# Key normalisation by pairs of heads, gate constants in their own memory, and two later places for small TensorE work in a one-core encoder layer

## The chip, the core and the metric

The kernel runs on one core of one Trainium2 chip. The metric is the device time of one execution in microseconds (us). The core's engines work side by side, each through a queue of its own in order: TensorE (PE) multiplies matrices and transposes; VectorE (DVE), ScalarE (ACT) and GpSimd (POOL) work on elements; SyncE (SP) issues most DMA transfers. An engine waits for another by semaphores.

## The reference

One layer of a hybrid encoder is computed for 1024 new frames and for 64 further frames of a stream with 512 cached ones; everything is float32.

```python
h = rms_norm(x, g_norm1) * (1 + scale1) + shift1
c_q, c_kv, k_rope_raw, gq, gk, gv, g_lr, g_r = split(h @ w_in)
# latent attention: 4 heads, key of 128 + 64 rotary, value of 128
latent = concat(past_latent, rms_norm(c_kv, g_kv_lora))
kv = (latent @ w_ukv).reshape(B, S, 4, 128 + 128)      # k_nope, v
k = concat(k_nope, krope);  k = rms_norm(k, g_k_head);  k = concat(k[:128], rope(k[128:]))
a_out = chunk_causal_attention(q, k, v)
# gated linear attention
log_a = log_sigmoid(g_lr @ w_gate_up + b_gate_up) / 16
b_out, s_new = gla(gq, gk, gv, log_a, s0), gated by silu(g_r)
x = x + gate1 * (concat(a_out, b_out) @ w_out)
h2 = rms_norm(x, g_norm2) * (1 + scale2) + shift2
x = x + gate2 * (square(relu(h2 @ w_up)) @ w_down)
```

## The kernel before, in words

Tokens lie along the free axis where a projection is multiplied, 1088 of them in chunks of 384, 384 and 320, later in halves of 544 and quarters of 272. Precise products are made by `mm3` (L94 to L96): each operand is split into a high and a low part, and three fast matmuls (high x high, low x high, high x low) are added in PSUM. The splitting is done by ACT (high part, a cast, L102) and DVE (low part, a subtraction, L103 and L106). PSUM is handed out in three groups of banks, named in the profile by the tile that a matmul writes: `mm` (four), `tp` (two) and `g` (two).

The stages follow one another with much overlap: the modulation vectors (`mod_vec`, L177), the first norm and the input projection; the gated linear attention (from about 90 us); the keys of the past and the queries (265 to 360 us); attention with the keys of the new tokens made along the way (to some 560 us); the output projection and the second norm (to 700 us); the MLP.

What a stage emits is decided by `interleave`. Streams are generators that yield three things: an estimate of PE time, a delay before they may go on, and a condition. `interleave` lets the first ready stream go on and moves a model clock. So the delays (`yield 0, 4500, None`, in model nanoseconds) say how much other work goes between two steps of a stream. The tile framework then sets the order within each engine's queue by an estimate of its own, so an edit in one place can move instructions in others.

Keys and values (`keys_values`, L960): for a tile of 128 tokens two products of the latent with the matrix `UK`, each for two heads, go into two `g` banks. From each, DVE copies the keys to `kn` (L982) and the values to `v` (L985), and ACT squares the keys and adds them up (L984, two per product). After both, POOL adds epsilon and the rotary part's square (L988) and raises to the power -1/2 (L989) for all four heads at once; DVE multiplies the keys (`kn`, L991) and the rotated part (`krt`, L992) by it, 128x512 each. Later, after the delay in L995, PE transposes `kn` (L998, four heads) and then `krt` (L1005). The function is used for four past tiles (t = 0 to 3), for the 64 new tokens of the running stream (`new_keys(8)`), both in `past_keys`, and for the eight tiles of new keys.

The gate of the linear attention: `wg` holds `w_gate_up` with its bias in row 96, and `glrT` the transposed low-rank input with a row of ones. Both are zeroed by POOL, and `wg`, its bias and the small indicator matrix `indi` are loaded, when the pool `big` is opened, whose memory is that of earlier tiles (L613 to L625). L653 transposes the input (from DVE's copy L650), L654 copies it into `glrT`, and L657 multiplies.

The second norm (`norm2`, L1471 to L1506) works on the four column blocks of 272 tokens in turn. `main` evicts each of the eight rows of the output projection with the residual added (L1456), ACT squares it (L1460, L1463) and DVE adds the squares to `acc` (L1464). After a delay (L1473) PE sums `acc` over partitions (L1478), DVE and POOL make the reciprocal root (L1481, L1482), DVE puts it on diagonals (L1485), and after a second delay PE broadcasts it (L1489).

## Time and profile before

| what | value |
|---|---|
| median of 3 runs | 1357.65 us (1357.14 to 1358.04) |
| profiled execution | 1358.17 us |
| its span, first to last instruction | 1356.4 us |
| mean granted TensorE clock | 0.996 |
| busy: PE, DVE, ACT, POOL | 1325.8, 894.9, 655.3, 64.5 us |
| DMA | 183.64 MB, mean 135 GB/s |

A row of the groups view has line, engine, operation, output <- input, shapes and count, then busy time and mean nanoseconds of one, then the idle time of the engine just before with what ended it. A row of the timeline has the start, the duration and in brackets the idle time before with its releaser. A row of the waits has the waiting engine and tile, the releaser, and us in total, times and the longest. A row of the windows has the stretch, its length, the busy time of PE, weight loads, DVE, ACT and POOL with counts, the granted clock, the DMA share and GB/s. Durations of pipelined matmuls overlap, so starts tell more than lengths.

### The profile page before, as it was taken

To read this page: it belongs to the slowest core of one execution; us is meant where nothing else is said; L and a number is where in the kernel's file an instruction comes from. 1 tells how busy PE (TensorE), PEld (TensorE's weight loads), DVE (VectorE), ACT (ScalarE), POOL (GpSimd) and SP (SyncE) were. 2 spreads that over 40 slices of the span, in tenths; PEclk is the share of its full clock that TensorE was granted. 3 is DMA by queue.
4 is the path that set the end of the run, shared out by engine and by line. 5 is a ranking of instruction groups with operands and counts; after the bars stand their busy time and mean duration, and the time that the engine had idled before them with its cause. 6 is when DMAs were issued, how large, how long until landed. Compare 5 with 4: busy or idle time off the path is not lost.

```text
span 1356.4 us, 25887 instructions
## 1 busy us (share of the span) xinstructions
PE 1325.8 (98%) x10052; PEld 1257.9 (93%) x10052; DVE 894.9 (66%) x1926; ACT 655.3 (48%) x1634; POOL 64.5 (5%) x110
## 2 busy tenths in 40 slices
PE   9999999989999999999989999999999999999998
PEld 8899999878867788999989999999999999999998
DVE  4898787465576656677799565665636865874554
ACT  5465545443255656753575445444443333433432
POOL 0110010121111100000000000000000000000000
PEclk9999999999999999999999999999999999999999
DMA  9420123324445320573417443444349845543441
GB/s 343 137 74 1 48 76 90 107 83 126 153 129 171 96 89 16 163 209 111 137 40 232 141 156 128 160 139 138 115 168 341 282 152 192 162 125 92 132 124 34
DMA packets 155110, 183.64 MB, mean 135 GB/s; under 512 B 16063, under 2 KB 106475, under 8 KB 154987
## 3 DMA queue, kind: packets, MB, share of 16 engines
q1 hardware_dynamic: 147530, 176.44, 41.0%
q10 hardware_dynamic: 7456, 5.54, 1.3%
q8 instruction: 79, 1.29, 0.4%
q14 instruction: 45, 0.36, 0.1%
HBM read 130.71 MB, written 51.23 MB: 134 GB/s over the span
## 4 chain that ended last, share of the span: by engine, by line
PE 82%; DVE 7%; DMA 4%; ACT 4%; POOL 2%; issue 1%; SPq 0%; ACTq 0%; DVEq 0%; POOLq 0%
PE mm L94 14%; PE mm L96 13%; PE mm L95 13%; PE g L94 6%; PE g L96 6%; PE g L95 6%; PE tp L94 3%; PE tp L95 3%; PE tp L96 3%; PE mm L1076 3%; PE g L1103 2%; PE mm L177 1%; PE g L881 1%; PE tp L1113 1%; POOL ssk L989 1%
## 5 line engine op out<-in xcount | busy, mean ns | idle before, releaser
L102 ACT CAST opers<-quad 128x512 fp32r<-128x512 f32 x112 | 69.4, 620 | 184.6 <-PE mm L96 145.1
L103 DVE TENSOR_TENSOR opers<-quad,opers 128x512 fp32r<-128x512 f32 x112 | 77.2, 690 | 112.3 <-ACT opers L102 112.3
L96 PE MATMUL mm<-opers 128*128 128x272 f32 x448 | 128.9, 288 | 0.0
L94 PE MATMUL mm<-opers 128*128 128x272 f32 x448 | 128.6, 287 | 0.3 <-DVE e L1910 0.3
L95 PE MATMUL mm<-opers 128*128 128x272 f32 x448 | 128.3, 286 | 0.0
L94 PE MATMUL mm<-ah,wh 128*128 128x272 f32 x424 | 122.5, 290 | 2.0 <-ACT wh L102 1.7
L95 PE MATMUL mm<-al,wh 128*128 128x272 f32 x424 | 121.8, 288 | 0.3 <-DVE al L103 0.3
L96 PE MATMUL mm<-ah,wl 128*128 128x272 f32 x424 | 121.6, 288 | 0.0
L94 PE MATMUL mm<-hh,wh 128*128 128x384 f32 (+2 forms) x264 | 90.6, 344 | 0.7 <-ACT wh L321 0.7
L95 PE MATMUL mm<-hl,wh 128*128 128x384 f32 (+2 forms) x264 | 87.2, 330 | 0.0
L96 PE MATMUL mm<-hh,wl 128*128 128x384 f32 (+2 forms) x264 | 86.9, 330 | 0.0
L94 PEld LDWEIGHTS mm<-opers 128*128 128x128 f32 x448 | 84.6, 189 | 0.5 <-issue 0.5
L96 PEld LDWEIGHTS mm<-opers 128*128 128x128 f32 x448 | 84.3, 188 | 0.0
L95 PEld LDWEIGHTS mm<-opers 128*128 128x128 f32 x448 | 84.1, 188 | 0.0
L94 PEld LDWEIGHTS mm<-ah,wh 128*128 128x128 f32 x424 | 80.0, 189 | 3.1 <-ACT wh L102 2.2
L95 PEld LDWEIGHTS mm<-al,wh 128*128 128x128 f32 x424 | 79.8, 188 | 0.5 <-DVE al L103 0.5
L96 PEld LDWEIGHTS mm<-ah,wl 128*128 128x128 f32 x424 | 79.8, 189 | 0.0
L103 DVE TENSOR_TENSOR opers<-ru,opers 128x544 fp32r<-128x544 f32 x108 | 77.6, 719 | 2.2 <-ACT opers L102 2.0
L102 ACT CAST opers<-ru 128x544 fp32r<-128x544 f32 x108 | 69.4, 643 | 13.1 <-PE mm L96 11.7
L102 ACT CAST wh<-ru 128x512 fp32r<-128x512 f32 x67 | 41.1, 618 | 65.7 <-PE g L95 24.6
L103 DVE TENSOR_TENSOR wl<-ru,wh 128x512 fp32r<-128x512 f32 x67 | 45.9, 689 | 35.5 <-ACT wh L102 35.3
L94 PE MATMUL mm<-wh,hh 128*128 128x264 f32 (+3 forms) x216 | 65.9, 305 | 0.0
(410 smaller groups left out, 4241.5 us busy)
## 6 DMA issues: line engine op xcount, KB each, us to landing
ru<-u_d SPq DMA_DIRECT2D x108, 272.0 KB, 2.9
raw<-in_w_ada SPq DMA_DIRECT2D x40, 512.0 KB, 4.2
ru<-in_w_up SPq DMA_DIRECT2D x32, 512.0 KB, 4.1
quad<-in_w_down SPq DMA_DIRECT2D x16, 1024.0 KB, 7.2
u_d<-st SPq DMA_DIRECT2D x60, 272.0 KB, 2.1
u_d<-sc SPq DMA_DIRECT2D x45, 272.0 KB, 2.2
raw<-in_w_in SPq DMA_DIRECT2D x22, 256.0 KB, 3.8
x<-in_xo_T SPq DMA_DIRECT2D x8, 544.0 KB, 6.1
```

Of the source, the lines that this page charges most:

```text
L94: pin(PE.matmul(out, lhsT=ah, rhs=bh, start=first, stop=False, skip_group_check=more))
L95: pin(PE.matmul(out, lhsT=ah, rhs=bl, start=False, stop=False, skip_group_check=more))
L96: pin(PE.matmul(out, lhsT=al, rhs=bh, start=False, stop=last, skip_group_check=more))
L102: ACT.copy(hi, src)
L103: eng.tensor_tensor(out=lo, in0=src, in1=f32(hi), op=ALU.subtract)
L177: mm = PE.matmul(acc[32 * j:32 * j + 32, 0:256], lhsT=scT[:, k, :], rhs=was[k][:, 256 * j:256 * (j + 1)], start=(k == 0), stop=(k == KT - ...
L881: PE.matmul(sc[:n, a, p], lhsT=d[:, w * p + n * a:w * p + n * a + n], rhs=qv[:, :, p, a], start=True, stop=True)
L989: POOL.tensor_tensor(out=ss[:n, 4:8], in0=ss[:n, 4:8], in1=mhalf[:n], op=ALU.pow)
L1076: PE.matmul(sp[:n, :w], lhsT=x[:, hd, :n], rhs=y[:, hd, :w], start=(j == 0), stop=(j == 4))
L1103: PE.matmul(op[:n, 0:P], lhsT=pt[:kw, k, :n], rhs=kvs[kt // 4].v[:kw, kt % 4, hd], start=(kt == 0), stop=(kt == nkt - 1))
L1113: PE.transpose(tp[:kw, k, :n], pr[k0 // 4][:n, P * k:P * k + kw], ident[:n, :n])
```

## The change

There are four edits. First, `wg`, the two `glrT` and `indi` get tiles of their own in the pool `gqkp`, which is open from the start; they are zeroed at the beginning of the program, and the three loads, of which two were issued by ACT, are issued by SP within `shifts`, after the third load of columns of x. Second, in `keys_values` POOL's addition and power are done for two heads after each product, and DVE's two multiplications become four of 128x256. Third, the delay before the transposes of `kn` becomes 7000 instead of 4500 for the past tiles and for `new_keys(8)`. Fourth, the delay before the second norm's sums becomes 4500 instead of 2500, except in the last column block. Lines behind the edits have numbers higher by 3 (L998 is L1001, L1478 is L1481).

```diff
@@ before the loaders
+    wg = gqkp.tile([97, 256], F32, name="wg")
+    POOL.memset(wg, 0.0)
+    glrT = [gqkp.tile([97, 320], F32, name=f"glrT{j}") for j in range(2)]
+    for t in glrT:
+        POOL.memset(t[0:96], 0.0)
+        POOL.memset(t[96:97], 1.0)
+    indi = gqkp.tile([P, 2], F32, name="indi")
@@ shifts()
             load_x(2)
+            SP.dma_start(wg[0:16], I["w_gate_up"])
+            SP.dma_start(wg[96:97], I["b_gate_up"])
+            SP.dma_start(indi, I["gla_ind"])
@@ the pool big
-        wg = big.tile([97, 256], F32, name="wg")
-        POOL.memset(wg, 0.0)
-        ACT.dma_start(wg[0:16], I["w_gate_up"])
-        SP.dma_start(wg[96:97], I["b_gate_up"])
-        glrT = [big.tile([97, 320], F32, name=f"glrT{j}") for j in range(2)]
-        for t in glrT:
-            POOL.memset(t[0:96], 0.0)
-            POOL.memset(t[96:97], 1.0)
-        indi = big.tile([P, 2], F32, name="indi")
-        ACT.dma_start(indi, I["gla_ind"])
@@ keys_values()
-    def keys_values(lh, ll, ki, tab, n, kv, slot):
+    def keys_values(lh, ll, ki, tab, n, kv, slot, ahead=4500):
...
             DVE.tensor_copy(kv.v[:n, slot, 2 * g:2 * g + 2], pg[:, :, P:2 * P])
+            POOL.tensor_scalar(out=ss[:n, 4 + 2 * g:6 + 2 * g], in0=ss[:n, 2 * g:2 * g + 2], scalar1=ss[:n, 8:9],
+                               scalar2=192 * EPS, op0=ALU.add, op1=ALU.add)
+            POOL.tensor_tensor(out=ss[:n, 4 + 2 * g:6 + 2 * g], in0=ss[:n, 4 + 2 * g:6 + 2 * g], in1=mhalf[:n, 0:2], op=ALU.pow)
             yield 1300, 0, None
-        POOL.tensor_scalar(out=ss[:n, 4:8], in0=ss[:n, 0:4], scalar1=ss[:n, 8:9], scalar2=192 * EPS, op0=ALU.add, op1=ALU.add)
-        POOL.tensor_tensor(out=ss[:n, 4:8], in0=ss[:n, 4:8], in1=mhalf[:n], op=ALU.pow)
-        rs = ss[:n, 4:8].rearrange("p (h o) -> p h o", o=1).broadcast_to([n, H, P])
-        DVE.tensor_tensor(out=kn[:n], in0=kn[:n], in1=rs, op=ALU.mult)
-        DVE.tensor_tensor(out=kr[:n], in0=R[:n].rearrange("p t d c -> p t (d c)").broadcast_to([n, H, P]),
-                           in1=rs, op=ALU.mult)
+        rs = [ss[:n, a:a + 2].rearrange("p (h o) -> p h o", o=1).broadcast_to([n, 2, P]) for a in (4, 6)]
+        for g in range(2):
+            DVE.tensor_tensor(out=kn[:n, 2 * g:2 * g + 2], in0=kn[:n, 2 * g:2 * g + 2], in1=rs[g], op=ALU.mult)
+        for g in range(2):
+            DVE.tensor_tensor(out=kr[:n, 2 * g:2 * g + 2], in0=R[:n].rearrange("p t d c -> p t (d c)").broadcast_to([n, 2, P]),
+                              in1=rs[g], op=ALU.mult)
         cs = slice(P * slot, P * slot + n)
-        yield 0, 4500, None
+        yield 0, ahead, None
@@ past_keys(), new_keys()
-            yield from keys_values(lh, ll, 8 + t, t, P, kvS[0], t)
+            yield from keys_values(lh, ll, 8 + t, t, P, kvS[0], t, 7000)
-            yield from keys_values(lh, ll, 12, 4, n, kvN[0], 0)
+            yield from keys_values(lh, ll, 12, 4, n, kvN[0], 0, 7000)
@@ norm2()
-                yield 0, 2500, None
+                yield 0, 2500 if end else 4500, None
```

Three places show how the order moves. The first is PE's queue at the second past tile, from the last product with `UK` (`latl` is the low part of its latent) to the transposes of `kn`; the numbers are the rows' places in the queue. Before:

```order
1292 L96 MATMUL g<-wh,latl 128x512
1293 L710 MATMUL tp<-ident,cn 128x128
1294 L96 MATMUL mm<-wh,hl 128x320
...
1310 L94 MATMUL mm<-wh,hh 128x320
1311 L95 MATMUL mm<-wl,hh 128x320
1312 L998 MATMUL tp<-ident,kn 128x128 x4
```

and in the changed kernel:

```order
1301 L96 MATMUL g<-wh,latl 128x512
1302 L96 MATMUL mm<-wh,hl 128x320
...
1309 L710 MATMUL tp<-ident,cn 128x128 x2
1310 L94 MATMUL mm<-wh,hh 128x320
...
1333 L96 MATMUL mm<-wh,hl 128x320
1334 L1001 MATMUL tp<-ident,kn 128x128 x4
```

The projection's matmuls between the product and the transposes went from 18 (1294 to 1311) to 31 (1302 to 1308 and 1310 to 1333).

The second is DVE's queue at the first tile of new keys, where the copies of `kn` and `v` empty the banks of the two products. Before:

```order
479 L982 COPY kn<-g 128x256 x2
480 L985 COPY v<-g 128x256
481 L957 TENSOR_TENSOR latl<-latr,lath 128x256
482 L985 COPY v<-g 128x256
483 L991 TENSOR_TENSOR kn<-kn,ssk 128x512
484 L992 TENSOR_TENSOR krt<-R,ssk 128x512
```

and in the changed kernel:

```order
490 L982 COPY kn<-g 128x256
491 L993 TENSOR_TENSOR kn<-kn,ssk 128x256
492 L985 COPY v<-g 128x256
493 L982 COPY kn<-g 128x256
494 L995 TENSOR_TENSOR krt<-R,ssk 128x256
495 L957 TENSOR_TENSOR latl<-latr,lath 128x256
496 L985 COPY v<-g 128x256
497 L993 TENSOR_TENSOR kn<-kn,ssk 128x256
498 L995 TENSOR_TENSOR krt<-R,ssk 128x256
```

The first pair's multiplication of `kn` now stands ahead of the first copy of `v` and of the second copy of `kn`.

The third is PE's queue at the second norm's first sums, from the end of one column block's output projection (`woh`, `wol`) into the next block's. Before:

```order
2772 L96 MATMUL mm<-mh_6878,wol 128x272
2773 L94 MATMUL mm<-mh_7173,wh 128x272
...
2796 L96 MATMUL mm<-mh_7173,wl 128x272
2797 L1478 MATMUL tp<-ones,acc 128x1 x2
2798 L1478 MATMUL tp<-ones,acc 16x1
```

and in the changed kernel:

```order
2779 L96 MATMUL mm<-mh_6930,wol 128x272
2780 L94 MATMUL mm<-mh_7225,wh 128x272
...
2815 L96 MATMUL mm<-mh_7225,wl 128x272
2816 L1481 MATMUL tp<-ones,acc 128x1 x2
2817 L1481 MATMUL tp<-ones,acc 16x1
```

The matmuls of the next block ahead of the sums went from 24 to 36.

## The prediction

> **What bounds the kernel now.** I read the busy table first, then the span in four windows, then the waits of TensorE, and only then single places.
>
> ```profile
> span 1356.4 us, 25887 instructions
> PE 1325.8 (98%) x10052; PEld 1257.9 (93%) x10052; DVE 894.9 (66%) x1926; ACT 655.3 (48%) x1634; POOL 64.5 (5%) x110
> ...
> 0.00:260.00 260.00, 252.39 (x1861) 234.35 (x1862) 191.98 (x450) 136.95 (x409) 21.66 (x42) 1.00 0.35 110
> 260.00:480.00 220.00, 208.89 (x1403) 170.20 (x1402) 136.85 (x372) 108.53 (x394) 33.68 (x54) 0.99 0.41 125
> 480.00:720.00 240.00, 231.82 (x1729) 221.05 (x1729) 171.36 (x421) 139.59 (x327) 9.16 (x14) 0.99 0.39 116
> 720.00:1356.00 636.00, 632.68 (x5066) 632.27 (x5064) 394.72 (x686) 270.25 (x504) 0.00 (x0) 1.00 0.48 157
> ```
>
> Columns of the windows: length, then busy PE, PEld, DVE, ACT, POOL, the granted clock, the DMA share. TensorE (PE) is the bound. Its idle time is 30.6 us in all, and 27 us of it lie before 720 us: 7.6 up to 260, 11.1 in 260 to 480, 8.2 in 480 to 720. The change adds no matmul, so it can only win this idle time, or time lost to a lower clock. The waits say whose it is:
>
> ```profile
> PE tp L998 <- DVE kn L991: 5.7, 5, 1.6
> PE tp L1113 <- ACT prob L1087: 3.5, 3, 1.2
> PE tp L1478 <- DVE acc L1464: 1.8, 1, 1.8
> PE mm L177 <- DMA raw<-in_w_ada: 1.2, 1, 1.2
> PE g L657 <- POOL SB L629: 1.1, 1, 1.1
> PE tp L710 <- DVE cn L696: 0.9, 1, 0.9
> ```
>
> Three of these (L998, L1478, L657) are what the edits touch. The clock is the second account:
>
> ```profile
> 404.00:406.00 2.00, 2.00 (x10) 1.67 (x10) 1.14 (x5) 1.06 (x4) 0.00 (x0) 0.50 0.50 129
> ...
> 594.00:596.00 2.00, 0.25 (x3) 0.28 (x3) 0.44 (x1) 2.00 (x3) 0.00 (x0) 1.00 1.01 338
> 596.00:598.00 2.00, 2.00 (x16) 1.96 (x17) 1.42 (x3) 0.11 (x1) 0.41 (x1) 0.88 1.09 372
> 598.00:600.00 2.00, 2.00 (x11) 2.00 (x11) 1.11 (x4) 0.43 (x1) 0.83 (x2) 0.50 1.11 279
> 600.00:602.00 2.00, 2.00 (x13) 1.85 (x13) 0.52 (x2) 0.19 (x1) 0.00 (x0) 0.77 0.63 208
> ...
> 704.00:706.00 2.00, 1.76 (x8) 1.44 (x8) 2.00 (x6) 0.81 (x2) 0.00 (x0) 0.50 0.36 139
> ```
>
> Behind the emptiest stretch of PE (0.25 us busy of 2) the clock is halved: (0.12 + 0.50 + 0.23) x 2 = 1.7 us of work lost in 596 to 602, all of it on the path, since PE is busy there. There are three such stretches: around 404, 599 and 705 us.
>
> **The change, part by part.** *Keys by pairs.* The chain behind the last UK product of the first past tile is:
>
> ```profile
> 269.88 0.42 DVE L982 COPY kn<-g 128x256 f32<-128x256 f32 x1
> ...
> 271.14 0.31 POOL L988 TENSOR_SCALAR ssk<-ssk 128x4 f32<-128x4 f32 x1 [3.70 <-ACT krt L984]
> 271.53 1.03 POOL L989 TENSOR_TENSOR ssk<-ssk,mhalf 128x4 f32<-128x4 f32 x1
> ...
> 272.60 0.69 DVE L991 TENSOR_TENSOR kn<-kn,ssk 128x512 f32<-128x512 f32 x1 [1.11 <-POOL ssk L989]
> ...
> 273.44 0.63 PE L998 MATMUL tp<-ident,kn 128*128 128x128 f32 x4 [1.58 <-DVE kn L991]
> ```
>
> Afterwards only the second pair hangs on the last product. The prices of the halves:
>
> ```profile
> L1482 POOL TENSOR_TENSOR st<-st,mhalf 128x2 f32<-128x2 f32 x3 | 2.1, 697 | 111.4 <-DVE st L1481 111.4
> L355 POOL TENSOR_TENSOR st<-st,mhalf 128x2 f32<-128x2 f32 x1 | 1.0, 999 | 0.9 <-DVE st L353 0.9
> ...
> L754 DVE TENSOR_TENSOR dd<-dd,gqk 128x256 f32<-128x256 f32 x28 | 11.8, 421 | 2.6 <-ACT dd L743 2.3
> ```
>
> A power of 128x2 took 0.70 to 1.00 against 1.03 for 128x4; I take 0.78, nearer the three rows. A multiplication of 128x256 takes 0.42 against 0.69. So the chain after the last product shortens by 0.25 + 0.27, with the smaller addition about 0.55 us (0.3 to 0.6). On DVE the four small multiplications cost 1.68 against 1.38, 0.3 us for each of 13 tiles, 4 us; on POOL some 0.8 us for each. Neither is on the path: in 260 to 480 us DVE is busy 137 and POOL 34 of 220 us, and that idle time is the cover. Without it the 4 us would be the price.
>
> *Past keys' transposes later.* By the order on PE, 31 instead of 18 matmuls of 128x320 stand between the last product and the second tile's transposes. A matmul of 128x272 takes 0.125 us in the last window, so 13 wider ones are at least 1.6 us. The stalls at L998 in the past tiles are 1.58, above, and these two:
>
> ```profile
> 283.85 0.63 PE L998 MATMUL tp<-ident,kn 128*128 128x128 f32 x4 [1.05 <-DVE kn L991]
> ...
> 295.48 0.63 PE L998 MATMUL tp<-ident,kn 128*128 128x128 f32 x4 [1.39 <-DVE kn L991]
> ```
>
> The second and third stalls vanish (-1.05, -1.39). The first tile's transposes keep 18 matmuls ahead of them, and gain the shorter chain and what goes between the pairs: about -1.0. Together -3.4 (bounds -2.4 and -4.0). The attention that reads these keys starts long after, so the delay costs nothing there.
>
> *New keys.* Here the order puts pair 0's transposes before the second pair's in some tiles, and pair 0's multiplication into DVE's queue ahead of evictions. Stalls of 0.89, 0.54 and 0.77 us at L998 lie at 388, 421 and 461 us:
>
> ```profile
> 388.00 0.66 PE L998 MATMUL tp<-ident,kn 128*128 128x128 f32 x4 [0.89 <-DVE kn L991]
> ...
> 421.46 0.66 PE L998 MATMUL tp<-ident,kn 128*128 128x128 f32 x4 [0.54 <-DVE ql L1052]
> ...
> 461.14 0.63 PE L998 MATMUL tp<-ident,kn 128*128 128x128 f32 x4 [0.77 <-DVE kn L991]
> ```
>
> I count -0.8, -0.5 and -0.75, and -0.5 at the softmax of 401.75 (1.07 us), where the sums on DVE stand behind both full multiplications. Against that, in tile 0 the new order makes a wait:
>
> ```profile
> 357.22 0.27 ACT L984 ACTIVATE krt<-g 128x128 f32<-128x128 f32 x1
> ...
> 358.77 0.36 PE L94 MATMUL g<-wh,cqh 128*64 128x384 f32 x1 [0.37 <-DVE v L985]
> ```
>
> Pair 0's squares end at 357.6. Addition 0.25, power 0.7 to 1.0, multiplication 0.42 give 359.1 to 359.4 for its transposes, which now stand before the query products that started at 358.77; and v's copy, which frees their bank, stands behind that multiplication. Less the 0.3 us of transposes done early, +0.7 (0.3 to 1.1). Tile 6 has a milder case, +0.4. Sum of new keys -1.45 (bounds -2.5 and 0).
>
> *Constants.* The gate product waits for its constants' space:
>
> ```profile
> 90.41 1.45 POOL L629 MEMSET SB<- 128x512 f32 x3
> ...
> 89.61 0.27 DVE L654 COPY glrT<-tp 16x128 f32<-16x128 f32 x1
> ...
> 91.14 0.27 DVE L654 COPY glrT<-tp 16x128 f32<-16x128 f32 x1
> 91.51 1.10 PE L657 MATMUL g<-glrT,wg 97*128 97x256 f32 x4 [1.06 <-POOL SB L629]
> ```
>
> The named releaser is the memset, but the product started right behind DVE's copy, which ended at 91.41. In the new order it stands ahead of the third transposition and needs an earlier copy (89.88): -0.9 (bounds 0 and -1.1). The three loads join SP's queue ahead of the past rows. An issue takes 0.43 us, 1.3 together, in front of weight rows that SP issues at 38.67 only when PE lets their buffer go; the stall they feed (L177, 1.19) comes four matmuls later in the order: -0.3 (bounds -0.7 and +0.6).
>
> *Second norm's sums.* Twelve more matmuls come first:
>
> ```profile
> 595.75 0.71 PE L1478 MATMUL tp<-ones,acc 128*128 128x1 f32 x6 [1.78 <-DVE acc L1464]
> ...
> 598.32 0.77 DVE L1485 TENSOR_SCALAR dg<-ident,st 128x128 f32<-128x128 f32 x3 [0.76 <-POOL st L1482]
> ```
>
> At 0.125 us each (632.68 us for 5066 in the last window) they cover 1.5 us, and 0.3 to 0.4 us of stall stays: -1.4 (bounds -0.5 and -1.8). What is late next is the broadcast L1489, which moves by the same twelve and keeps 24 matmuls, 3.0 us, behind the sums; from the sums' end, 596.46, to the last diagonal, 599.09, took 2.6 us here.
>
> *Clock.* With 0.3 to 0.4 us of idling in place of 1.78 the stretch at 599 goes: -1.7. The one at 404 followed the softmax stall, half of which I count as gone: half of 1.7, -0.85. The one at 705 stays (bounds -1.7 and +1.7: the order at the start of the MLP shifts too). That a stall need not halve the clock is seen behind the 1.39 us of the third past tile:
>
> ```profile
> 296.00:298.00 2.00, 1.87 (x14) 1.60 (x13) 1.61 (x6) 1.51 (x4) 0.00 (x0) 1.00 0.21 70
> ```
>
> [...]
>
> The sum is -3.4 - 1.45 - 0.9 - 0.3 - 1.4 - 2.55 = -10.0. I give back 1 us for bank waits at L710, which now stands right beside the moved transposes (such waits reach 0.9 us above): -9.0. The profiled execution took 1358.17 us, 1.8 over its span and 0.5 over the median 1357.65. That makes 1349.2 for it and 1348.7 for the median.
>
> **The rivals.** *The stalls go, the slow stretches stay or fall elsewhere.* For: three longer stalls passed without halving, so place and moment matter, and all moments shift. Against: the lowered windows stand right behind the emptiest ones. Then -6.4: 1351.2. [...]
>
> *The time is given back later.* For: the attention has waits the change doesn't touch (L1113, 3.5 us, and a transfer at 423 us), and what arrives earlier may wait longer there. Half of the sum or less: 1353 to 1357. Against: from 720 us PE has no gap to fill, and before, most waits are for short chains that move along with PE.
>
> *Slower, by pair 0 at DVE's head.* DVE takes its queue in order. If pair 0's multiplication, waiting for POOL, holds back copies in most tiles as in new tile 0, each costs 0.7 to 1.1 us, and an added halving 1.7. It decides from about 11 tiles at 0.9 (9.9 us): 13 tiles and one halving are +13.4 - 9.0, 1362. Against: in the past tiles PE has 18 to 36 matmuls of other work ahead, and I find the tight order in two new tiles only.
>
> **How the numbers follow.** No change means within 0.2%, 1354.9 to 1360.4, about what a measurement can tell. Forecast (up to 1350.5) 0.5; stalls without the clock (to 1353) 0.2; time given back 0.22, of which 0.11 still faster and 0.11 not to be told; slower 0.08, with 0.02 of it inside the band. So faster 0.81, same 0.13, slower 0.06. All terms at their far ends (-4.0, -2.5, -1.8, -1.8, -3.4) would be 1344; a tenth lies below that, and up to 1355.5 leaves a tenth above.
>
> **What would show it.** L998's 5.7 us of waits falls to 1 to 2 us; L1478 waits under 0.6 us and the clock is 1.00 behind it; L657 has no wait; a new wait of 0.7 to 1.1 us stands before the query products of new tile 0; DVE's busy time grows by about 4 us and POOL's by about 10. Wrong would be: L998 waiting as long as before, the sums' stall moved to L1489, or halved stretches behind new stalls.

## The result, and the profile after

The changed kernel took 1351.76 us (median of 7 executions, 1351.43 to 1355.38) beside 1357.65 us for the kernel before (7 executions, 1355.59 to 1361.91): a ratio of 0.9964, interval 0.9950 to 0.9978. Run again later beside another set of executions it took 1351.96 us (11 executions) against 1357.55, ratio 0.9960 (0.9947 to 0.9972). The change is faster by 5.6 to 5.9 us. The forecast was 9.0 us less, 1348.7, with a range of 1344.0 to 1355.5: the side and the range hold, the size does not.

The head of the page of the changed kernel, with busy time and instruction counts:

```profile
span 1350.0 us, 25954 instructions
...
PE 1322.5 (98%) x10052; PEld 1254.7 (93%) x10052; DVE 895.6 (66%) x1952; ACT 654.8 (49%) x1634; POOL 74.9 (6%) x136
```

The same four windows as before (length, then busy PE, PEld, DVE, ACT, POOL, granted clock, DMA share, GB/s):

```profile
0.00:260.00 260.00, 254.13 (x1869) 235.44 (x1869) 192.61 (x451) 137.15 (x410) 21.53 (x42) 1.00 0.35 110
260.00:480.00 220.00, 211.58 (x1436) 173.53 (x1435) 139.35 (x402) 111.49 (x404) 44.18 (x80) 1.00 0.42 127
480.00:720.00 240.00, 231.84 (x1753) 221.49 (x1751) 176.16 (x427) 141.57 (x328) 9.14 (x14) 1.00 0.40 119
720.00:1350.00 630.00, 624.91 (x5002) 624.28 (x5000) 387.45 (x673) 264.61 (x493) 0.00 (x0) 1.00 0.47 156
```

PE's idle time went from 30.6 to 27.5 us, only 3.1 less, and the clock is 1.00 in every window. In the third window PE idles as long as before (8.2 us). The waits of PE in the changed kernel (us in total, times, longest):

```profile
PE tp L1001 <- DVE kn L993: 2.4, 3, 1.2
...
PE mm L94 <- ACT st L1703: 1.4, 1, 1.4
PE tp L1008 <- ACT cl L713: 1.3, 1, 1.3
PE tp L1481 <- DVE acc L1467: 1.2, 1, 1.2
...
PE mm L177 <- DMA raw<-in_w_ada: 0.4, 1, 0.4
...
PE g L657 <- DVE glrT L654: 0.3, 1, 0.3
```

The wait for the keys fell from 5.7 to 2.4 us, the one for the sums from 1.8 to 1.2, and the gate product waits no more for the memset. New are 1.3 us at L1008 and 1.4 us at L94 behind L1703, at 731.57 us.

**A ledger between the same matmuls.** Idle time in fixed windows misleads here, since the work slides through the windows. All kernels of this study run the same 10052 matmuls, and the edits only reorder them within certain stretches. So I cut the sequence where the stretches end: between two cuts every kernel here has the same set of matmuls, and the time from the first start to the last can be set side by side. One profiled execution each, in us, worked out from the starts of the matmuls in the trace; a star marks each 3.41 us of halved clock that lies in the section:

```
matmuls      what lies there                   before   change   again    difference (change)
0-640        start, norm, projection            83.71    84.29    84.11    +0.58
640-900      gate of the linear attention       36.25    35.09    35.09    -1.16
900-1900     linear attention, projection      146.03   145.63   145.75    -0.40
1900-2300    past keys                          71.55    69.46    69.67    -2.09
2300-2800    queries, first new keys            75.89*   73.94    74.22    -1.95
2800-3150    new keys and attention             51.11    50.58    50.42    -0.53
3150-4000    attention, output projection      118.64   118.07   117.98    -0.57
4000-4600    output projection, norm's sums     79.67*   77.40    77.26    -2.27
4600-5200    start of the MLP                   82.69*   84.70    84.45*   +2.01
5200-10051   the rest of the MLP               606.11   606.11   606.11     0.00
```

The differences add up to -6.4 us, as do those of the two spans (1356.4 and 1350.0). Three things stand out. The MLP's bulk is the same to 0.01 us. The start of the MLP became 2.0 us longer. And two of the three sections with a gain of about 2 us are those that lost a halved stretch. The sums' section and the start of the MLP together took 162.4 us before and 162.1 after: what is won in the first is lost in the second.

**The clock over many executions.** Each execution comes with its span and its mean granted clock (three decimals, so a halving of 1.7 us shows as 0.001). Span x (1 - clock) is the time lost to the lower clock if PE is busy throughout. Over 92 executions the kernel before loses 5.07 us on the mean, two to three halvings and the run's end (in the profiled execution the clock is halved in the last 1.1 us of the span), and takes 1352.70 beside that; over 18 executions the changed kernel loses 1.35 and takes 1350.92 (standard errors 0.2 and 0.3 us for the lost clock, 0.1 and 0.3 for the rest). So of the mean gain of 5.5 us, 3.7 are clock and 1.8 are everything else, with each halving at its full price. The price can be read from the same executions: with 1 us more of lost clock the time is longer by 0.93 us in the kernel before (0.08 standard error) and by 0.56 in the changed one (0.18), whose one profiled halving lies at the start of the MLP (e12). By these prices 4.0 of the 5.5 us are clock. The spread of the kernel before, from 1352.3 to 1362.6, follows largely from it: the number of halvings differs from execution to execution (correlation 0.78).

### The profile page after: what moved, and what is told of

The parts are those of the page before. It is cut to its first block, busy times and chain, and to the rows that moved or that the text cites. A ratio compares the mean times of both kernels' runs of the same rounds, so it can differ in the third digit from the quotient of the medians.

```text
span 1350.0 us, 25954 instructions
## 1 busy us (share of the span) xinstructions
PE 1322.5 (98%) x10052; PEld 1254.7 (93%) x10052; DVE 895.6 (66%) x1952; ACT 654.8 (49%) x1634; POOL 74.9 (6%) x136
## 4 chain that ended last, share of the span: by engine, by line
PE 82%; DVE 8%; DMA 3%; ACT 3%; issue 2%; POOL 1%; SPq 0%; ACTq 0%; DVEq 0%; POOLq 0%
PE mm L94 14%; PE mm L96 14%; PE mm L95 14%; PE g L94 5%; PE g L96 5%; PE g L95 5%; PE mm L1079 3%; PE tp L94 3%; PE tp L96 3%; PE tp L95 3%; PE g L1106 2%; PE g L881 2%; PE tp L1116 1%; PE mm L177 1%; DVE al L103 1%
## 5 line engine op out<-in xcount | busy, mean ns | idle before, releaser
L94 PE MATMUL mm<-opers 128*128 128x272 f32 x448 | 128.5, 287 | 0.3 <-DVE e L1913 0.3
L94 PE MATMUL mm<-ah,wh 128*128 128x272 f32 x424 | 122.2, 289 | 4.1 <-ACT wh L102 2.3
L94 PE MATMUL mm<-hh,wh 128*128 128x384 f32 (+2 forms) x264 | 91.1, 346 | 0.7 <-ACT wh L328 0.7
L94 PEld LDWEIGHTS mm<-opers 128*128 128x128 f32 x448 | 84.6, 189 | 0.5 <-issue 0.5
L94 PEld LDWEIGHTS mm<-ah,wh 128*128 128x128 f32 x424 | 79.8, 188 | 5.4 <-ACT wh L102 3.0
L94 PE MATMUL mm<-wh,hh 128*128 128x264 f32 (+3 forms) x216 | 65.7, 304 | 0.0
```

The lines of the kernel that those rows point to most:

```text
L94: pin(PE.matmul(out, lhsT=ah, rhs=bh, start=first, stop=False, skip_group_check=more))
```

## The experiments

The experiments take single edits out of the changed kernel (e1 to e4), put single edits into the kernel before (e10, e11), or try a cause (e5 to e9). All ratios are against the kernel before.

### e1: constants back

```diff
-    wg = gqkp.tile([97, 256], F32, name="wg")
...
-            SP.dma_start(wg[0:16], I["w_gate_up"])
...
+        wg = big.tile([97, 256], F32, name="wg")
+        POOL.memset(wg, 0.0)
+        ACT.dma_start(wg[0:16], I["w_gate_up"])
...
```

> The changed kernel with its first edit undone: wg, glrT and indi are again zeroed and loaded when the pool 'big' opens. Theory (each edit changes only its own part of the queues, and the waits there are what it is worth): the wait for w_ada returns from 0.41 to 1.2 us and the gate product's 1.06 us returns, less 0.3 us of small waits that are new now: +1.2 to +1.8 us on the changed kernel, about 1353.2 where the clock is never halved, and nothing changes behind 260 us but by a shift. Rival (what is won there is waited for later in the linear attention): within 0.5 us of the changed kernel.

Measured: 1353.19 us (1350.34 to 1357.83, 12 executions), ratio 0.9969 (0.9957 to 0.9981). The interval overlaps that of the whole change, so this edit's worth, 1.2 us by the medians, isn't told from nothing. The gate's wait is back; the one for `w_ada` rose only from 0.4 to 0.7 us, not to the 1.2 expected:

```profile
PE g L657 <- POOL SB L629: 1.0, 1, 1.0
```

The ledger shows why 1 us of wait is not 1 us of time. Matmuls 640 to 900 took 35.09 to 35.11 us in every kernel with the constants in their own place and 36.25, 36.28, 36.18 and 35.73 in the four with the old place: the edit wins 1.1 us there (0.6 against the last of them). But matmuls 0 to 640 took 82.7 to 83.7 us with the old place (four kernels) and 83.3 to 84.6 with the new one (nine): it loses about as much on the mean, though the ranges overlap, with no wait to show for it. With the edit the scheduler also orders PE otherwise there: the weight products (L177) are cut differently around the first norm's diagonals. PE's timeline with the old place:

```profile
49.15 0.64 PE L177 MATMUL mm<-raw,scT 128*32 128x256 f32 x8
...
50.17 0.83 PE L362 MATMUL g<-dg,ones 128*128 128x128 f32 x6
50.76 0.42 PE L96 MATMUL mm<-hh,wl 128*128 128x384 f32 x1
```

and in the changed kernel:

```profile
49.91 0.62 PE L177 MATMUL mm<-raw,scT 128*32 128x256 f32 x2
50.46 0.94 PE L369 MATMUL g<-dg,ones 128*128 128x128 f32 x6
51.32 0.63 PE L177 MATMUL mm<-raw,scT 128*32 128x256 f32 x6
51.88 0.44 PE L94 MATMUL mm<-hh,wh 128*128 128x384 f32 x1
```

Eight weight products in a row took 0.57 us from the first start to the next row's; two and six apart took 0.55 and 0.56, and the diagonals 0.86 instead of 0.59. That is 0.8 us at this place, and 0.6 at a second one like it at 53.13 us. All of it counts as busy.

### e2: pairs back

```diff
-            POOL.tensor_scalar(out=ss[:n, 4 + 2 * g:6 + 2 * g], ...
-            POOL.tensor_tensor(out=ss[:n, 4 + 2 * g:6 + 2 * g], ..., op=ALU.pow)
...
+        POOL.tensor_scalar(out=ss[:n, 4:8], in0=ss[:n, 0:4], scalar1=ss[:n, 8:9], ...
+        POOL.tensor_tensor(out=ss[:n, 4:8], in0=ss[:n, 4:8], in1=mhalf[:n], op=ALU.pow)
...
+        DVE.tensor_tensor(out=kn[:n], in0=kn[:n], in1=rs, op=ALU.mult)
```

> The changed kernel with the normalisation of all four heads at once, as before; the later transposes of the past keys stay. Theory: the first past tile waits about 1.6 us (1.15 with pairs), the waits of 0.5 to 0.9 us at the transposes of new tiles 2, 4 and 7 return, the softmax wait near 400 us returns to about 1.1, the new wait of 0.87 us at new tile 0 falls to 0.4: +1.3 to +2 us, about 1353.4 without halvings. Rival (the prediction's sizes): +2.5 us or more. Rival (the pairs' own waits and what they displace cancel the gain): within 0.5 us.

Measured: 1355.38 us (1352.88 to 1357.04, 12 executions), ratio 0.9977 (0.9965 to 0.9989), 3.4 us over the second run of the whole change, more than the theory's 1.3 to 2. PE's wait for the keys:

```profile
PE tp L998 <- DVE kn L991: 3.0, 3, 1.3
```

The past keys took 70.01 us (69.46 with pairs), so the pairs are worth 0.5 us there beside the longer delay. Matmuls 2300 to 2800 took 75.76 against 73.94, and the clock was halved at 400.1 us. Of 13 profiled executions (those of e5 aside), the three with all four heads at once (before, this one, e10) have a halving in that section and the ten with pairs have none. The lost clock over 12 executions is 3.4 us on the mean against 1.35.

### e3: key delay back

```diff
-            yield from keys_values(lh, ll, 8 + t, t, P, kvS[0], t, 7000)
+            yield from keys_values(lh, ll, 8 + t, t, P, kvS[0], t)
...
-            yield from keys_values(lh, ll, 12, 4, n, kvN[0], 0, 7000)
+            yield from keys_values(lh, ll, 12, 4, n, kvN[0], 0)
```

> The changed kernel with the delay ahead of the past keys' transposes at 4500 again, pairs kept. Theory: with pairs the second and third past tile wait 0.5 to 0.8 us each, and the 1.30 us wait that the delay has put before the rotated keys of the second tile goes: net +0 to +1 us, 1351.8 to 1352.8. Rival (the prediction's sizes: the delay alone removes 1.05 and 1.39 us): +1.3 us or more, 1353 or above.

Measured: 1352.60 us (1350.31 to 1355.14, 12 executions), ratio 0.9963 (0.9950 to 0.9975): no difference to the whole change. PE's wait for the keys:

```profile
PE tp L1001 <- DVE kn L993: 4.3, 7, 1.0
```

The waits for `kn` rise from 2.4 to 4.3 us, but the 1.3 us at L1008 are gone. Past keys: 70.04 against 69.46. Pairs alone or delay alone bring the 71.55 us of before to 70.0; both together to 69.5.

### e4: sums' delay back

```diff
-                yield 0, 2500 if end else 4500, None
+                yield 0, 2500, None
```

> The changed kernel with the delay ahead of the second norm's sums at 2500 again. Theory (from 560 to 735 us VectorE, ScalarE and transfers set the pace, so the time that TensorE wins at the sums is waited for again at the start of the MLP): the wait at the sums is about 1.8 us again, the waits between 675 and 735 us together are 1 to 2.5 us shorter, and the time is within 0.7 us of the changed kernel, plus 1.7 us for each halving of the clock, which the longer wait makes likelier: 1351 to 1353.5. Rival (the prediction: the edit is worth 1.4 us of waiting and a halving): 1354.5 or above, with the waits between 675 and 735 us as in the changed kernel.

Measured: 1354.90 us (1352.15 to 1355.93, 12 executions), ratio 0.9979 (0.9969 to 0.9990), 2.9 us over the second run of the whole change. The wait of before is back:

```profile
PE tp L1481 <- DVE acc L1467: 1.8, 1, 1.8
```

The mean time is thus where the rival had it, but beside the clock nothing differs. The mean lost clock is 3.61 us without the delay and 1.35 with it, and what remains is 1351.03 without and 1350.92 with. The ledger agrees: the sums' section took 78.19 us here with no halving, 0.8 more than with the delay, and the start of the MLP 84.13 (one halving), 0.6 less; the waits between 675 and 735 us are 4.7 us instead of 5.9, as the theory had it.

### e5: how empty must PE be?

Twenty-one waits in the down projection, made with 2, 4 or 7 copies on DVE that the next matmul has to wait for, gave 4 gaps of 1.1 us, 9 of 2.8 to 3.6 and 8 of 4.6 to 4.8.

```diff
+                    idle = j in (3, 7, 11)
+                    if idle:
+                        for _ in range({3: 2, 7: 4, 11: 7}[j]):
+                            DVE.tensor_copy(junk, banks[3, 1])
...
```

> The changed kernel with 21 waits put into the dense last stage: at steps 3, 7 and 11 of each of the seven products of the down projection VectorE copies one bank 2, 4 or 7 times before TensorE may add to it again. By the 0.38 us of such a copy, TensorE idles some 1.1, 1.9 and 3.0 us or more, seven times each, between dense matmuls. Theory (the clock is judged in stretches of 3.41 us that lie on a fixed grid, and a stretch with too little work halves the next one): all halvings start a multiple of 3.41 us apart; none follows the short waits, some of the middle ones by where the grid falls, nearly all of the long ones, 8 to 12 in all, each costing 1.7 us. Rival (only a stretch of 3.4 us without any work halves): none behind short and middle waits, at most two behind long ones. Rival (any wait over 1 us halves): 20 or more.

Measured: 1457.46 us in one execution, a clock of 0.973. All waits as one group:

```profile
PE mm L94 <- DVE junk L1886: 69.7, 21, 4.8
```

The 8 long gaps were all followed by a halving, 7 of the 9 middle ones, none of the short ones: 15 halvings, more than the 8 to 12 expected, and neither rival's number. The record of the granted clock in the traces has a grain that I had not looked for. Its halved stretches, in us from the span's start:

```
kernel      start and length of the halved stretches (the run's end left out)
before      402.96 3.41     597.52 3.41     703.34 3.41
change      none
e10         388.77 6.83
e11         590.62 6.83
e5          695.59 3.41    1040.33 3.41    1057.40 6.83    1088.12 3.41    1105.18 6.83  ...
```

Every length is a multiple of 3.413 us. So are the distances between starts: 194.56 and 105.82 in the kernel before are 57.0 and 31.0 times 3.413, and all of e5's starts fit one such grid. The grid lies differently in the four executions of this table that have a halving: its first line is 0.2, 3.1, 0.1 and 2.7 us behind the span's start. So in these traces the clock changes window by window, and whether a halving follows a gap goes with how the gap falls across the windows. I cut the ten traces that have a halving by their own grid and took PE's busy share of each window and whether the next one was halved (windows already at half left out):

```
busy share of the window     next window halved
under 0.40                   21 of 21
0.40 to 0.65                  5 of 41
0.65 to 0.75                  3 of 57
over 0.75                     0 of 3806
```

A gap of 3.55 us in e5 that lay across two windows (1.88 and 1.67 us) halved nothing; the 1.78 us at the sums, with further idling and small matmuls in the same window, did. Busy share alone does not decide between 0.40 and 0.75 (halved at 0.74, not halved at 0.45); what else counts is open.

### e6: sums still later

```diff
-                yield 0, 2500 if end else 4500, None
+                yield 0, 2500 if end else 7000, None
```

> The changed kernel with the delay ahead of the sums at 7000 instead of 4500: 53 instead of 36 matmuls stand before them. Both theories have the wait at the sums (1.19 us) go. Theory (VectorE sets the pace from 680 to 705 us, so what is won at the sums is waited for later): the time beside halvings stays within 0.4 us of the changed kernel's 1351.1, and the waits between 675 and 735 us grow by about what the sums no longer wait. Rival: -1.0 to -1.2 us, with those waits unchanged.

Measured: 1357.34 us (median of 12, of which one at 4028 us stands alone; the others 1354.29 to 1358.55), ratio 0.9992 (0.9982 to 1.0002). The whole gain is gone, which neither theory nor rival had. The sums no longer wait, the broadcast does:

```profile
598.27 1.24 POOL L1485 TENSOR_TENSOR st<-st,mhalf 128x2 f32<-128x2 f32 x2 [66.45 <-DVE st L1484]
599.00 0.77 DVE L1488 TENSOR_SCALAR dg<-ident,st 128x128 f32<-128x128 f32 x3 [0.76 <-POOL st L1485]
...
599.44 0.92 PE L1492 MATMUL tp<-dg,ones 128*128 128x128 f32 x4 [3.03 <-DVE dg L1488]
```

Between sums and broadcast too little other work is left, and the chain over DVE and POOL stands bare. Behind its 3.03 us the clock was halved at 599.7, and twice more later; the start of the MLP took 86.73 us.

### e7: the MLP's sums on POOL

The start of the MLP is where the time was given back, and DVE is busy without a break there. The windows of the changed kernel from 685 us:

```profile
685.00:690.00 5.00, 5.00 (x42) 4.99 (x40) 5.00 (x9) 4.05 (x12) 0.00 (x0) 1.00 0.00 0
690.00:695.00 5.00, 2.76 (x19) 2.24 (x17) 5.00 (x13) 3.34 (x9) 0.00 (x0) 1.00 0.36 105
695.00:700.00 5.00, 4.34 (x30) 3.83 (x30) 5.00 (x15) 2.35 (x5) 0.00 (x0) 1.00 0.16 59
700.00:705.00 5.00, 4.60 (x33) 3.96 (x32) 5.00 (x12) 2.88 (x7) 0.00 (x0) 1.00 0.38 109
```

POOL is idle meanwhile. So the three sums over 128x1088 that `sums_of` makes (L1395 to L1397) were given to it.

```diff
-        DVE.tensor_tensor(out=X[21][:, :, hs], in0=X[21][:, :, hs], in1=X[22][:, :, hs], op=ALU.add)
-        sub(X[12][:, :, hs], X[12][:, :, hs], X[22][:, :, hs], DVE)
+        POOL.tensor_tensor(out=X[21][:, :, hs], in0=X[21][:, :, hs], in1=X[22][:, :, hs], op=ALU.add)
+        sub(X[12][:, :, hs], X[12][:, :, hs], X[22][:, :, hs], POOL)
...
```

> The changed kernel with the three elementwise operations of sums_of (128x1088 each, 1.28 us on VectorE, twice in the program) issued by GpSimd, which is idle there. Theory (VectorE is the bound from 680 to 705 us): 2.5 to 3.8 us of its work leave the stretch, and the time falls by 0.5 to 2.5 us, with shorter waits of TensorE between 680 and 735 us, unless GpSimd's operations hold VectorE's up. Rival (VectorE is busy but not what TensorE waits for): no change within 0.5 us. Rival (both engines hold each other up, as the additions of 128x2 on GpSimd showed, 0.53 us beside a VectorE multiplication and 0.30 without): the same or slower, with VectorE's operations lengthened there.

Measured: 1355.87 us (11 executions), ratio 0.9983 (0.9971 to 0.9994), some 4 us slower than the change. The timeline:

```profile
680.66 2.52 POOL L1395 TENSOR_TENSOR x<-x,x 128x1088 f32<-128x1088 f32 x1 [8.41 <-ACT x L1500]
681.12 2.60 DVE L103 TENSOR_TENSOR wl<-tw,wh 128x512 fp32r<-128x512 f32 x1 [0.31 <-ACT wh L102]
683.14 2.96 POOL L106 TENSOR_TENSOR x<-x,x 128x1088 f32<-128x1088 f32 x1
683.65 3.00 DVE L103 TENSOR_TENSOR wl<-ru,wh 128x512 fp32r<-128x512 f32 x1
```

DVE's subtraction of 128x512 takes 0.69 us in the changed kernel (at 681.45 us) and 2.60 to 3.00 here: each ends 0.5 us after the POOL instruction that it meets, about its own length, as if it could only run behind it. The work left DVE and its time did not (900.6 us busy instead of 895.6), as the rival that has both engines hold each other up said. The clock was halved for 10.24 us from 684.7, and over the executions 5.78 us of clock are lost. Beside that the kernel takes 1349.8 us, less than the change's 1350.9, so whether the moved sums cost time other than through the clock isn't shown.

### e8: the addition on DVE

In the changed kernel POOL's addition of two elements should take 0.3 us. Beside DVE's multiplications it does not:

```profile
268.68 0.47 POOL L986 TENSOR_SCALAR ssk<-ssk 128x2 f32<-128x2 f32 x1 [2.22 <-ACT krt L984]
...
270.31 0.42 DVE L995 TENSOR_TENSOR krt<-R,ssk 128x256 f32<-128x256 f32 x1
...
270.41 0.53 POOL L986 TENSOR_SCALAR ssk<-ssk 128x2 f32<-128x2 f32 x1 [0.48 <-ACT krt L984]
...
271.02 0.71 POOL L988 TENSOR_TENSOR ssk<-ssk,mhalf 128x2 f32<-128x2 f32 x1
...
357.58 0.30 POOL L986 TENSOR_SCALAR ssk<-ssk 128x2 f32<-128x2 f32 x1 [1.88 <-ACT krt L984]
```

Of the 26 additions, the 9 that began while a DVE instruction with two inputs in SBUF had 0.09 us or more to run took 0.47 to 0.85 us. The other 17 took 0.29 to 0.30, also one in which such an instruction began 0.09 us later and one that began 0.03 us before the end of one. Among these 17 are additions beside a copy out of PSUM (L985) and one that began while a DVE instruction with only one of its two inputs in SBUF (L1010) had 0.25 us to run. So this kernel makes the addition on DVE:

```diff
-            POOL.tensor_scalar(out=ss[:n, 4 + 2 * g:6 + 2 * g], in0=ss[:n, 2 * g:2 * g + 2], scalar1=ss[:n, 8:9],
+            DVE.tensor_scalar(out=ss[:n, 4 + 2 * g:6 + 2 * g], in0=ss[:n, 2 * g:2 * g + 2], scalar1=ss[:n, 8:9],
...
```

> The changed kernel with the pairs' addition (128x2) on VectorE instead of GpSimd; the power stays on GpSimd. Theory (the addition is held up on GpSimd by VectorE's multiplication of the other pair, 0.53 us instead of 0.30, which eats the pairs' gain): the chain behind the last product of the first past tile becomes 0.3 to 0.5 us shorter, its wait falls from 1.15 to 0.6 to 0.85 us, and the time beside halvings falls by 0.5 to 1.5 us over the 13 tiles. Rival (the addition waits in VectorE's queue as long as it was held up before): no change within 0.4 us.

Measured: 1352.85 us (10 executions), ratio 0.9965 (0.9953 to 0.9976): no difference to the change. The addition took 0.22 us, but it stood in DVE's queue:

```profile
270.52 0.20 ACT L984 ACTIVATION_READ_ACCUMULATOR krt<-g 128x1 f32 x1
...
271.77 0.22 DVE L986 TENSOR_SCALAR ssk<-ssk 128x2 f32<-128x2 f32 x1
272.07 0.74 POOL L988 TENSOR_TENSOR ssk<-ssk,mhalf 128x2 f32<-128x2 f32 x1 [1.48 <-DVE ssk L986]
```

The last square ended at 270.72 us and the addition began at 271.77, so the chain of the first past tile was not shorter but longer (5.60 us instead of 4.83, from the start of the last product), and its wait 1.12 us instead of 1.15, not the 0.6 to 0.85 of the theory. The past keys took 0.9 us less all the same (68.53 against 69.46), because two other waits of PE went, 0.43 us at L1153 and 0.78 at L710, and one of 0.31 came. Matmuls 2300 to 2800 took 0.8 us longer and 3150 to 4000 1.0 longer. PE's order changed in the first of these two, but not in the second, so PE's order isn't the whole of it.

### e9: without the MLP's sums

```diff
     def sums_of(hs):
-        DVE.tensor_tensor(out=X[21][:, :, hs], in0=X[21][:, :, hs], in1=X[22][:, :, hs], op=ALU.add)
...
+        pass
```

> The changed kernel without the three elementwise operations of sums_of (it leaves out the sums of the second norm's rows that stand for part of the MLP's precision scheme, so other numbers come out; the time shows what those operations cost). They are 3.8 us of VectorE's work in the full stretch 680 to 705 us and as much near 626 us. Theory (VectorE is the bound from 680 to 705 us): the time beside halvings falls by 1.5 to 3 us, to 1348 to 1349.6, and TensorE's idle time between 670 and 740 us from 6.0 to 3 to 4.5 us. Rival (TensorE waits there for something else): idle time and time within 0.5 us of the changed kernel.

Measured: 1347.13 us (1345.94 to 1348.61, 4 executions), ratio 0.9921 (0.9898 to 0.9944), 3.7 us below the 1350.9 that the change takes beside the lost clock, and below the theory's 1348 to 1349.6. The start of the MLP took 80.51 us instead of 84.70: 4.2 us less, for 6.5 us of DVE's work (889.1 busy instead of 895.6). PE fills up, and DVE stays full:

```profile
690.00:695.00 5.00, 3.90 (x29) 3.46 (x28) 5.00 (x15) 3.29 (x7) 0.00 (x0) 1.00 0.35 105
695.00:700.00 5.00, 4.51 (x34) 4.29 (x35) 5.00 (x11) 2.57 (x5) 0.00 (x0) 1.00 0.51 155
```

So DVE's work is on the path here. The scheduler's order of PE changed along with it from matmul 4830 on, so a part of the 4.2 us may be order.

### e10: only the sums' delay

The kernel before, with the fourth edit alone:

```diff
-                yield 0, 2500, None
+                yield 0, 2500 if end else 4500, None
```

> The kernel before with only the delay ahead of the second norm's sums raised to 4500. Theory (the edit is worth halvings alone): the mean of time less lost clock stays at the 1352.7 of the kernel before within 0.5 us; the clock lost falls from 5.1 to 2.5 to 4 us; the mean time falls by 1 to 2.5 us. Rival (the sums' wait is worth its length, halvings are chance): time less lost clock falls by 0.6 to 1.4 us, the lost clock stays at 5.

Measured: 1356.20 us (1353.52 to 1359.57, 12 executions), ratio 0.9989 (0.9976 to 1.0002): not told from no change. Beside the lost clock (3.84 us) it takes 1352.50, as before (1352.70). The sums' wait:

```profile
PE tp L1478 <- DVE acc L1464: 1.5, 1, 1.5
```

The sums' section fell to 77.73 us, with no halving (before: 79.67 with one), and the start of the MLP rose from 82.69 to 83.77.

### e11: only the pairs

The kernel before, with the second edit alone; the delay stays 4500:

```diff
+            POOL.tensor_scalar(out=ss[:n, 4 + 2 * g:6 + 2 * g], ...
+            POOL.tensor_tensor(out=ss[:n, 4 + 2 * g:6 + 2 * g], ..., op=ALU.pow)
...
```

> The kernel before with only the normalisation by pairs. Theory (from taking the edit out of the changed kernel: 0.7 us of waits and 2.0 us of halvings): time less lost clock falls by 0.3 to 1.3 us, the lost clock from 5.1 to 2.5 to 4 us, the mean time by 1.5 to 3.5 us. Rival (the prediction: waits are the larger part): time less lost clock falls by 2 us or more.

Measured: 1353.70 us (1350.96 to 1356.67, 12 executions), ratio 0.9972 (0.9960 to 0.9985). Beside the lost clock (3.27 us) it takes 1350.49, 2.2 less than before: all that the whole change has outside the clock, and the rival's mark rather than the theory's 0.3 to 1.3. The past keys took 70.00 us, with the wait for `kn` of e3 (4.3 us, 7 times). The sums waited longer:

```profile
PE tp L1481 <- DVE acc L1467: 2.2, 1, 2.2
```

Behind the sums' 2.2 us the clock was halved for two windows (6.83 us from 590.6), and that section took 81.56 us.

### e12: the change again

The changed kernel as it is, beside e9 to e11.

> The changed kernel once more, for more executions beside the same runs of the kernel before. Theory: mean 1352.4 within 0.7 us, lost clock 1 to 2 us, time less lost clock 1351.1 within 0.5 us; against the kernel before 1.5 to 2 us in time less lost clock and 3 to 4.5 us in lost clock. Rival (the few halvings of the changed kernel so far were chance): lost clock 3 us or more.

Measured: 1351.96 us (1350.58 to 1354.60, 11 executions), ratio 0.9960 (0.9947 to 0.9972). Its profiled execution has a halving at 695.8 us, where the first one had none, and still the start of the MLP took 84.45 us against 84.70. Together with the kernel before, whose 82.69 us hold one too and are the shortest of all kernels that make the sums, and with e4 and e11, which have one order of the queues there and took 84.13 us with a halving and 83.85 without, that says: a halving in this stage costs little or nothing. That PE would have waited there anyway is the likely reason.

## Why the prediction was right or wrong, by its steps

**Right: what bounds the kernel, and that the change wins.** PE's idle time and its clock were the two accounts, and the gain lies in both.

**Right in size: the keys.** The past keys were put at -3.4 with 1.0 given back for bank waits beside the moved transposes, -2.4 net; the ledger has -2.1. The inside was less right. The third stall did go, and the first fell to 1.15 us; but the second, which "vanishes", came back one instruction later. The moved transposes of `krt` (L1008) wait for a bank that ACT frees:

```profile
287.94 0.37 ACT L713 ACTIVATE cl<-tp,vT 128x128 f32<-128x128 f32 x1
288.37 0.66 PE L1008 MATMUL tp<-ident,krt 128*128 128x128 f32 x4 [1.30 <-ACT cl L713]
```

And the chain behind the last product shortened by 0.2 us instead of 0.55: from 268.41 to 273.44 before (5.03 us), from 267.42 to 272.25 after (4.83). The product before, and the chain after:

```profile
268.41 0.40 PE L96 MATMUL g<-wh,latl 128*128 128x512 f32 x1
```

```profile
267.42 0.40 PE L96 MATMUL g<-wh,latl 128*128 128x512 f32 x1
...
269.23 0.41 DVE L982 COPY kn<-g 128x256 f32<-128x256 f32 x1
...
271.76 0.42 DVE L993 TENSOR_TENSOR kn<-kn,ssk 128x256 f32<-128x256 f32 x1 [0.57 <-POOL ssk L988]
...
272.25 0.44 PE L1001 MATMUL tp<-ident,kn 128*128 128x128 f32 x2 [1.15 <-DVE kn L993]
```

Two terms were left out. The second addition took 0.53 instead of 0.30 us, beside DVE's new multiplication of the first pair's rotary part. And the second copy of `kn` began 1.81 us behind the start of the product instead of 1.47 (269.88 before), since two of DVE's 128x512 subtractions (L106) now stand ahead of it instead of one. Nine of the 26 additions were lengthened like that (0.47 to 0.85 us, under e8), and under e7 POOL lengthened DVE's subtractions (2.60 to 3.00 us instead of 0.69).

**Right in sum: new keys and the stretch at 404.** -1.45 and -0.85 were forecast, -2.3; matmuls 2300 to 3150 gave -2.5. The wait in new tile 0 came as worked out: 0.87 us, at 356.21 us, before the query products, and it cancels the stall that left (matmuls 2300 to 2700 took 59.97 us before and 60.04 after). The halving went whole (1.7 us) instead of by half, so the waits gave some 0.8 us instead of 1.45: the sum is right partly by luck.

**Wrong: constants and `w_ada`, -1.2.** The gate's stall gave 1.1 us as forecast. The loads were put at -0.3, with a far end of +0.6, by the queue they join. The wait that they feed did fall, from 1.2 to 0.4 us in the profiled pair. But the new order of PE cost more in the section ahead, in busy time: 1.4 us at the two places shown under e1, and 1 us net over the section (the means are 83.1 us with the old place and 84.1 with the new one). What is left is 0.6 us in the profiled pair and 0.1 by those means. The step that failed is that a moved load was judged by its queue alone; the order of the matmuls around it wasn't priced.

**Mis-sized: the sums, -1.4.** Twelve more matmuls took 0.6 us off the wait (1.78 to 1.19), and 0.8 off the section (78.19 in e4 to 77.40). I counted the cover as if `acc` were ready at the same moment. It is not: the square on ACT that `acc` needs stands behind an operation that waits for a transfer, before and after:

```profile
593.70 1.11 ACT L1267 ACTIVATE mr<-mr 128x1088 f32<-128x1088 f32 x1 [1.99 <-DMA mr<-r_d]
```

```profile
588.50 1.11 ACT L1270 ACTIVATE mr<-mr 128x1088 f32<-128x1088 f32 x1 [2.16 <-DMA mr<-r_d]
...
589.96 0.44 DVE L1467 TENSOR_TENSOR acc<-acc,sq 128x272 f32<-128x272 f32 x1 [2.74 <-ACT sq L1466]
...
590.55 0.71 PE L1481 MATMUL tp<-ones,acc 128*128 128x1 f32 x6 [1.19 <-DVE acc L1467]
```

That L1478 would wait under 0.6 us was wrong for this reason; that the clock behind it would be 1.00 was right.

**Wrong: nothing is given back behind the sums.** The range of rivals had this case, but put it in the attention, and against it I held that the waits ahead of 720 us are for short chains that move along with PE. The start of the MLP went from 82.69 to 84.70 us. From matmul 4000 to 5200, sums and start together, the delay won little or nothing: 162.4 us before and 161.5 with it alone (e10), 162.3 with the change but without it (e4) and 162.1 with it. With the pairs alone (e11), where the clock was halved for two windows behind the sums, it was 165.4.

The 2.0 us come in two halves. Matmuls 4680 to 4870 took 26.65 us in the three kernels with the old delay (before, e4, e11) and 27.67 to 27.70 with the new one (e6, e7 and e9 differ in more there). The delay has put the same matmuls in another order, and at matmul 4796 PE now meets a wait that the old order does not have:

```profile
681.47 0.40 PE L94 MATMUL mm<-ah,wh 128*128 128x272 f32 x1 [0.96 <-ACT wh L102]
```

It has nothing to do with coming earlier. PE reaches matmul 4680 at 665.6 us in the change and at 671.8 in e10, and both take 27.7 us; e4 reaches it at 667.3 and takes 26.65. The wait stays without the MLP's sums, too (0.87 us in e9, whose 26.76 us come from other waits). So this half is again the price of an order that I didn't price.

The other half lies in matmuls 4870 to 5200, which took 45.95 us before and 46.95 after; their largest wait is the new one of 1.4 us at 731.57. Here coming earlier does count. The kernels before, e11 and e4 have one order of all queues in this stage, and took 45.95, 47.12 and 47.40 us from 700.62, 696.82 and 693.97 us on; the change, e2 and e10 have another, and took 46.95, 46.29 and 46.00 from 693.25, 696.81 and 699.48 on. What is won before is waited for here in part. DVE, busy without a break for 20 us, is the likely cause, since e9 took 43.66 us; what sets the pace in detail is open. And the halved stretch at 705, for which I counted no change, lay where PE would likely have had to wait anyway.

**The clock, -2.55.** The mean over many executions is -3.7. In the profiled pair the two halvings that left were worth about 1.5 (sums) and 1.7 us (404). The step was too local: I priced the three stretches that one execution showed, while they are draws, since the grid of windows lay elsewhere in each of the four executions under e5. What the change seems to do is to leave fewer stretches with so much idling that the grid can catch them. A window need not be empty for it: the 21 windows with PE under 40% busy were followed by a halved one every time, and at the sums a gap of 1.78 us was enough, in a window with PE 52% busy.

**Other marks.** POOL's busy time grew by 10.4 us, as said. DVE's grew by 0.7 instead of 4: the multiplications' durations do add up to 4.0 us more, but neighbours overlap (a 128x256 takes 0.42 us, and the next one started 0.34 us behind it, at 269.97 and 270.31), and the durations of DVE's other instructions add up to 1.8 us less. The waits at L998 fell to 2.4 us, not to 1 to 2.

**The sum.** Against -9.0, the ledger has -6.4 (the terms here are rounded): 2.0 from the start of the MLP, 0.8 from the sums and their clock, 0.6 from the loads and 0.3 from the past keys are missing, and 1.2 came unforecast (0.2 in the new keys, 0.4 in 900 to 1900 and 0.6 in 3150 to 4000; PE has one order in these last two in every kernel here, and their times differ by as much among them). The first rival's time, 1351.2, is close to what was measured, but its mechanism is not: the slow stretches did go.

## What to carry to other kernels

Price a change between the same instructions, not by idle time in fixed windows: here a wait of 1.1 us went and left little gain, since the new order cost about as much in busy time ahead of it, and 2.0 us came back at the start of the MLP, half by a wait that a new order made and half where earlier work waits longer. When an edit moves the order in a queue, look at each stretch that moved. Look also for the next stage in which an engine other than the bound one is busy without a break; what arrives there earlier may wait there. And where the clock is lowered in some stretches, count them over many executions, because a profile shows one draw.

## What the runs showed of the hardware

- Every halved stretch of the granted clock but the one at the run's end lasted 3.413 us or a multiple of it, on a grid whose first line lay 0.1 to 3.1 us behind the span's start in four executions. Windows of this grid with PE under 40% busy were followed by a halved one in 21 of 21 cases, those over 75% in none of 3806, those in between in 8 of 98.
- An instruction of POOL and one of DVE with two SBUF inputs held each other up: a DVE subtraction of 128x512 took 2.60 to 3.00 us instead of 0.69 beside POOL sums of 2.5 to 3.0 us, and POOL's addition of 128x2 took 0.47 to 0.85 us instead of 0.30 in the 9 of 26 cases in which it began while one had 0.09 us or more to run. Beside nothing but DVE's copies out of PSUM it took 0.29 to 0.30. POOL's power of 128x2 took 0.69 to 0.73 us in the change; only three of the 26 began while such an instruction had 0.09 us or more to run, and took 0.71 and 0.73.
- The same 8 weight products of 128x256 with 32 columns took 0.57 us in a row and 1.11 us as 2 and 6.
